# A recurrence in units of two head pairs by a quarter of the tokens, with r, k and v kept in DRAM

## The chip, the cores and the metric

The kernel runs on one core of a Trainium2 chip. The time is device microseconds for one execution; the smaller, the better. The profile follows one execution instruction by instruction on the engines PE (matrix multiply; PEld is its weight load), DVE (VectorE), ACT (ScalarE), POOL (GpSimd) and SP (SyncE, which here only issues DMAs). Every engine works through its own queue of instructions in order.

## The reference

One layer over 1024 tokens of width 1024: a normalised and modulated input `h`, one wide projection, two groups of heads side by side, a gate on each, and an output projection. The first group is a recurrence over the tokens with a 64 x 64 state for each of 8 heads; the second is causal attention with low-rank queries, keys and values.

```python
h = rms_norm(x, norm_g) * (1 + scale) + shift
proj = h @ w_in
# 8 heads of 64: r, k, v, decay w, kk (normalised k) and a from proj
def step(state, inp):
    sa = einsum('bhvk,bhk->bhv', state, kk_t)
    state = state * w_t - sa * (kk_t * a_t) + v_t * k_t
    y = einsum('bhvk,bhk->bhv', state, r_t)
# group norm of y per head, + (r k r_k) v; attention heads beside it
y = concat([y_rwkv * silu(gate_r), y_mla * silu(gate_m)])
out = rms_norm(x + gate * (y @ w_out), final_g)
```

## The kernel before

**Stages.** (1) Loads, normalisation and modulation; the modulated input is held transposed as a high and a low part (`hTh`, `hTl`), and three tiles of the projection (the low-rank columns, k and r of the first head pair) are formed as it arrives. (2) The other 24 tiles of the input projection, with the recurrence woven between them. (3) `values`: value, rotary query and first key and query tiles for the attention. (4) Attention over four head pairs. (5) Output projection, final norm, stores.

**A projection tile** (`proj`, `mm3`) is 128 columns by 1024 tokens, made in two halves of 512 tokens. A half is 8 contraction blocks of three matmuls of 512 columns (high x high, high x low, low x high; lines 159 to 161, tile `mm`), in one of two PSUM banks. Afterwards an evacuation empties the bank: for r, k and v that is `evac_shift` (ACT line 211, DVE lines 212 and 218), which mixes each token with the one before it. In the kernel before, it writes tiles of its own (`rkv_`, six buffers for r and k, four for v) that stay in SBUF until the recurrence reads them. Others go through `etile`, three shared buffers of 128 x 512, and from there by DMA to DRAM.

**The recurrence in chunks.** It is not run token by token. A unit is one head pair by 512 tokens, so there are 8 units (4 pairs, 2 halves), each of 8 chunks of 64 tokens. For a unit, `prep` builds decays and scaled keys, `products` multiplies them (tile `gps`, line 552), `invert` inverts the triangular part of each chunk on DVE with 62 short instructions (lines 600, 602) between two trips through DRAM, `tmat` completes the inverse (`y1ps`, `y2ps`), and `turn_kb` and `turn_v` turn the operands. Then `chain` steps through the 8 chunks, and `post` normalises and gates what it gave.

**A step of the chain** is serial. First leg: X from the state (line 668), copied by ACT (672). Second leg: the inverse times X (679), two negating copies on ACT (685, 686); the old state goes through an identity matmul into the new one's bank (682). Third leg: the keys' part is added (690), and two scaled copies on ACT (693, 694) put the next state into `ST`. The output `Y` gets its two parts from lines 676 and 696. "Two" stands for the two heads of the pair, which lie on partitions 0 to 63 and 64 to 127. A step handles one chunk of one pair, so 64 steps follow in all; the chains of the four pairs don't depend on each other, but run one after another.

**What sets the order.** The main loop has 11 rounds `n` of `STEPS[n]` places. Tables give the place at which each piece of work is emitted (`PREP`, `PROD`, `TURN`, `TMAT`, `POST`); one leg of the chain is emitted at each place; and `RATE[n]` pieces of projection (one contraction block, three matmuls) go into each place from the generator `filler`, which takes the tiles in the order of the list `tiles` and then `values`. Unit n is prepared in round n, turned in round n+1, stepped through in round n+2, and finished in round n+3. A scheduler then orders the instructions of each engine by this order of emission, raised for evacuations (`first`) and for the chain's ACT copies (`quick`).

Of the kernel before, what the change touches and what calls it, by code (L numbers as in the profile page):

```python
# [17 lines left out]
F32 = mybir.dt.float32  # L18
# [4 lines left out]
ALU = mybir.AluOpType  # L23
# [4 lines left out]
P = 128  # L28
# [19 lines left out]
BKR = 6  # L48
BV = 4
# [8 lines left out]
PREP = ((0, 0, 1, 2, 3, 5, 5, 7), (4, 4, 5, 6, 7, 9, 9, 11), (9, 9, 10, 11, 12, 14, 14, 16))  # L58
PROD = ((8, 13), (12, 15), (17, 21))
TURN = (2, 5, 6)  # L60
POST = (1, 1, 5, 5, 8)
TMAT = ((13, 15), (14, 15), (15, 17))
EVAC = 120
STEPS = (16, 16, 24, 24, 24, 24, 24, 24, 24, 24, 9)
RATE = (2.3, 2.3, 2, 2, 2.2, 2, 2, 2, 1.7, 0.4, 1)
# [17 lines left out]
def hymba_kernel(ctx: ExitStack, tc: tile.TileContext, x, pos, cols, cst, winit, w_ada, b_gate, w_in, w_lora, w0,  # L83
# [38 lines left out]
    d_bv = [dram.tile([P, S], F32, name=f"d_bv{p}") for p in range(NP)]  # L122
    d_y = [dram.tile([P, S], F32, name=f"d_y{p}") for p in range(NP)]
# [63 lines left out]
    rkv = {}  # L187
# [11 lines left out]
    def evac_shift(ti, dest):  # L199
# [4 lines left out]
        def f(h, ps):  # L204
            if dest is None:
                o = etile("pst")
            else:
                o = (vp if dest[1] == "v" else rkvp).tile([P, HALF], F32, tag="v" if dest[1] == "v" else "kr", name=f"rkv_{dest}_{h}",
                              bufs=BV if dest[1] == "v" else BKR)
                rkv[dest + (h,)] = o  # L210
# [8 lines left out]
            if dest is None:  # L219
                hs = slice(h * HALF, (h + 1) * HALF)  # L220
                A.activation(LW[0:64, hs], o[0:64], AF.Tanh)
                A.copy(LW[64:128, hs], o[64:128])
# [18 lines left out]
    GROUP = [(O_LORA, evac_shift(12, None)), (RW, evac_shift(4, (0, "k"))), (0, evac_shift(0, (0, "r")))]  # L241
# [103 lines left out]
    def shift_tile(p, nm):  # L345
        ti = {"r": 0, "k": 4, "v": 8}[nm] + p
        return proj(ti * P, P, evac_shift(ti, (p, nm)))
# [113 lines left out]

    def prep(un):

        p, h = un["p"], un["h"]
        hs = slice(h * HALF, (h + 1) * HALF)
        cp = slice(p * P, (p + 1) * P)
        r, k = (rkv.pop((p, n, h)) for n in "rk")
        wl = tm.tile([P, P], F32, tag="wl", name="wl", bufs=2)
        SY.dma_start(wl[:], w_lora[:, cp])
        w0b = tm.tile([P, P], F32, tag="w0b", name="w0b", bufs=2)  # L470
        SY.dma_start(w0b[:], w0[:, cp].to_broadcast([P, P]))
        sq = t2("sq", (P, HALF))
        A.activation(sq[:], k[:], AF.Square, scale=col("k_k", p))
# [3 lines left out]
        T.matmul(aps[:], lhsT=wl[64:128], rhs=LW[64:128, hs], start=True, stop=True)  # L477
        for i in range(4):
            T.matmul(ps[:, i, :], lhsT=LW[0:64, h * HALF + i * P:h * HALF + (i + 1) * P], rhs=wl[0:64],
                     start=True, stop=True)  # L480
        z = t2("z", (P, 4, P))
        V.tensor_tensor(z[:], ps[:], w0b[:, None, :].to_broadcast([P, 4, P]), ALU.add)
        ta = t2("ta")
        A.activation(flat(ta), aps[:], AF.Tanh, scale=0.5, bias=a0h[:, p:p + 1])
# [15 lines left out]
        V.tensor_scalar(kw[:], ta[:], kah[:, p:p + 1], kam[:, p:p + 1], ALU.mult, ALU.add)  # L500
# [12 lines left out]
        yield  # L513
        ps = psA.tile([P, HALF], F32, tag="rp", name="kps")
# [3 lines left out]
        V.scalar_tensor_tensor(flat(kn), k[:], col("k_k", p), ps[:], ALU.mult, ALU.mult)  # L518
# [8 lines left out]

        V.scalar_tensor_tensor(flat(kw), r[:], col("r_k", p), flat(kw), ALU.mult, ALU.mult)
# [4 lines left out]
        V.tensor_tensor(kb[64:128, :, 1, :], kn[64:128], Ei[64:128], ALU.mult)  # L533
        yield
        ps = psA.tile([P, HALF], F32, tag="rp", name="bps")
        T.matmul(ps[:], lhsT=cs("blk"), rhs=flat(kw), start=True, stop=True)
        v = rkv.pop((p, "v", h))
        bv = t2("bv0", (P, HALF))
        V.tensor_tensor(bv[:], ps[:], v[:], ALU.mult)
        SY.dma_start(d_bv[p][:, hs], bv[:])  # L540
        un.update(eL=eL, rq=rq, kb=kb, v=v, GA=[[None, None], [None, None]])
        yield

    def products(un, q):

        p, h, kb, rq = un["p"], un["h"], un["kb"], un["rq"]
# [7 lines left out]
        dn = d_n[2 * p + h][:].rearrange("(s q c b) i j -> s q b i c j", s=2, q=2, b=2)  # L554
# [33 lines left out]
    def invert(un):  # L588

        i = 2 * un["p"] + un["h"]  # L590
# [16 lines left out]
    def fetch(un):  # L607

        i = 2 * un["p"] + un["h"]
        TT = un["TT"] = TTs[un["h"]]  # L610
# [37 lines left out]
    @contextmanager  # L648
    def quick(un):
        with tc.high_priority(offset=QUICK[un["p"] == NP - 1]):  # L650
            yield

    def chain(un, nxt):

        p, h = un["p"], un["h"]
# [3 lines left out]
        if h == 0:  # L659
            G.memset(ST[0:64, 0, 0, :], 0.0)  # L660
            G.memset(ST[64:128, 0, 1, :], 0.0)
        rcs = psA.tile([P, 2, 3, C], F32, tag="rc", name="rc", bufs=1)
        Y = un["Y"] = psA.tile([P, 8, C], F32, tag="ry", name="Y", bufs=1)
        for c in range(8):
            ps = rcs[:, c % 2]
            last = c == 7 and nxt is None
            for s in range(2):
                T.matmul(ps[rows[s], 0, :], lhsT=GA[s][c // 4][:, c % 4, 0:C], rhs=ST[:, c, s, :],  # L668
                         start=True, stop=True)
            X = ch.tile([P, C], F32, tag="X", name="X", bufs=2)  # L670
            with quick(un):
                A.copy(X[:], ps[:, 0, :])
# [240 lines left out]
    def filler():  # L913
        ws = [tiles[0][0]()]
        gr, tb = gate_row(), tables()
        for i, (_, steps) in enumerate(tiles):
# [5 lines left out]
            if i == 11:  # L922
                yield from scale_ckv()
# [411 lines left out]
```

## Time and profile before

| | us |
|---|---|
| three runs, median | 945.38 (942.20 to 951.51) |
| the profiled execution's own time | 947.39 |
| its span, first to last instruction | 945.6 |
| PE busy in it | 850.4 (90%) |
| DVE busy | 576.5 (61%) |
| ACT busy | 476.7 (50%) |
| POOL busy | 294.1 (31%) |

A busy PE is one with a matmul in flight, not one at its peak. A row of the timeline gives the start in us from the span's start, the time from first to last moment of the instructions that it merges, the engine, the line, and what was written and read; an engine's idle time ahead of it stands in brackets with what released it. A matmul of f32 data counts as two instructions, so that `x4` is two matmuls. The spacing from one row's start to the next is what a matmul costs in a row of others, since they overlap.

### The profile page before, as it was taken

What the parts mean: (1) busy time and instruction counts of PE and PEld (TensorE: products, weight loads), DVE (VectorE), ACT (ScalarE), POOL (GpSimd) and SP (SyncE); (2) the same over time, 40 slices, a digit from 0 to 9 for tenths busy, and PEclk for the clock granted to TensorE, in tenths of its full rate; (3) what the DMA queues carried; (4) which work ended last, traced back from release to release, by engine and by line L of the source; (5) the groups of instructions that cost most, each with busy time, mean ns of one, the idle gap of its engine ahead of it and who ended that gap; (6) DMA issues with size and microseconds to landing.
All of it is one profiled execution on the core that took longest, in us unless ns stands there. A gap on an engine that the chain in (4) does not pass through costs nothing.

```text
span 945.6 us, 16387 instructions
## 1 busy us (share of the span) xinstructions
PE 850.4 (90%) x5828; PEld 638.6 (68%) x5828; DVE 576.5 (61%) x1438; ACT 476.7 (50%) x1132; POOL 294.1 (31%) x355
## 2 busy tenths in 40 slices
PE   1799998999889999999999899896899998989897
PEld 1587776776667567667776666663677777868685
DVE  5796484293863855936636736462678778764333
ACT  2656131535635535445435444564688788762311
POOL 2314131133222322412325130323346454464300
PEclk9999998799999999999999999797899999999899
DMA  8762313124413424232332543335202031026133
GB/s 270 228 183 73 84 29 87 57 68 107 143 37 98 138 68 124 72 81 86 90 85 63 140 123 87 113 103 150 54 26 71 26 101 57 1 89 223 56 115 130
DMA packets 116737, 93.01 MB, mean 98 GB/s; under 512 B 38952, under 2 KB 92464, under 8 KB 116656
## 3 DMA queue, kind: packets, MB, share of 16 engines
q1 hardware_dynamic: 115696, 88.82, 32.0%
q0 software_dynamic: 960, 3.15, 1.4%
q8 instruction: 46, 0.75, 0.3%
q14 instruction: 35, 0.29, 0.1%
HBM read 69.12 MB, written 22.81 MB: 97 GB/s over the span
## 4 chain that ended last, share of the span: by engine, by line
PE 54%; DVE 17%; ACT 9%; DMA 7%; issue 5%; POOL 5%; SPq 1%; POOLq 0%; DVEq 0%; ACTq 0%
PE mm L159 8%; PE mm L160 6%; PE mm L161 6%; DVE W L602 3%; DVE wtmp L600 3%; DMA wor<-in_w_out 2%; PE tp L1052 2%; ACT pr L1041 2%; PE gps L552 2%; PE po L1114 2%; PE po L1116 2%; PE po L1115 2%; PE Y L676 2%; ACT PTh L1061 1%; PE rc L668 1%
## 5 line engine op out<-in xcount | busy, mean ns | idle before, releaser
L159 PE MATMUL mm<-hTh,whi 128*128 128x512 f32 (+1 forms) x384 | 171.8, 447 | 1.9 <-DVE tg L230 1.9
L160 PE MATMUL mm<-hTl,whi 128*128 128x512 f32 (+1 forms) x384 | 154.2, 402 | 0.0
L161 PE MATMUL mm<-hTh,wlo 128*128 128x512 f32 (+1 forms) x384 | 154.2, 401 | 0.0
L152 POOL TENSOR_TENSOR wlo<-wraw,whi 128x512 fp32r<-128x512 f32 (+1 forms) x54 | 69.8, 1293 | 206.8 <-ACT whi L151 192.3
L159 PEld LDWEIGHTS mm<-hTh,whi 128*128 128x128 f32 (+1 forms) x384 | 72.3, 188 | 23.6 <-issue 2.3
L161 PEld LDWEIGHTS mm<-hTh,wlo 128*128 128x128 f32 (+1 forms) x384 | 72.3, 188 | 17.8
L160 PEld LDWEIGHTS mm<-hTl,whi 128*128 128x128 f32 (+1 forms) x384 | 72.8, 190 | 12.4 <-issue 1.4
L1045 POOL TENSOR_SCALAR pr<-pr,sm 128x512 f32<-128x512 f32 (+2 forms) x96 | 55.2, 584 | 77.4 <-DVE sm L1042 50.0
L602 DVE TENSOR_TENSOR W<-W,wtmp 128x60 f32<-128x60 f32 (+24 forms) x248 | 68.8, 277 | 6.0
L600 DVE TENSOR_TENSOR wtmp<-W,N 128x60 f32<-128x60 f32 (+24 forms) x248 | 66.1, 267 | 7.0 <-DMA N<-d_n 0.9
L1041 ACT ACTIVATE pr<-sp,mx,rss 128x128 f32<-128x128 f32 (+3 forms) x64 | 53.3, 833 | 15.4 <-DVE mx L1034 13.0
L1062 DVE TENSOR_TENSOR PTl<-tp,PTh 128x512 fp32r<-128x512 f32 (+2 forms) x96 | 52.4, 554 | 12.2 <-ACT PTh L1061 10.1
L151 ACT CAST whi<-wraw 128x512 fp32r<-128x512 f32 (+1 forms) x54 | 32.6, 605 | 51.6 <-PE mm L160 45.1
L1033 DVE TENSOR_REDUCE mx<-sp 128x1 f32<-128x128 f32 (+3 forms) x64 | 48.0, 750 | 13.4 <-PE sp L1027 13.3
L1114 PE MATMUL po<-wo,yh 128*128 128x512 f32 x128 | 51.7, 404 | 3.9 <-DVE xo L1247 3.1
L1061 ACT CAST PTh<-tp 128x512 fp32r<-128x512 f32 (+2 forms) x96 | 44.0, 477 | 14.4 <-PE tp L1052 10.6
L1115 PE MATMUL po<-wo,yh 128*128 128x512 f32 x128 | 51.2, 400 | 0.0
L1116 PE MATMUL po<-wo,yl 128*128 128x512 f32 x128 | 51.2, 400 | 0.0
L1052 PE MATMUL tp<-cstt,pr 128*128 128x128 f32 x288 | 44.9, 278 | 4.4 <-POOL pr L1045 2.1
L1073 PE MATMUL op<-PTh,Vt 128*128 128x256 f32 (+1 forms) x160 | 41.9, 292 | 5.1 <-ACT od L1088 5.1
L685 ACT ACTIVATE ST<-rc 64x64 f32<-64x64 f32 x64 | 13.8, 215 | 52.7 <-PE rc L682 44.7
L1023 PE MATMUL sp<-kt,qt 96*128 96x512 f32 (+2 forms) x96 | 36.4, 379 | 4.2 <-ACT pr L1041 4.2
(394 smaller groups left out, 1974.7 us busy)
## 6 DMA issues: line engine op xcount, KB each, us to landing
wraw<-in_w_in SPq DMA_DIRECT2D x52, 256.0 KB, 3.0
wa<-in_w_ada SPq DMA_DIRECT2D x64, 128.0 KB, 3.4
xt<-in_x SPq DMA_DIRECT2D x8, 512.0 KB, 5.8
wg<-in_w_ada SPq DMA_DIRECT2D x32, 128.0 KB, 2.2
N<-d_n SPq DMA_DIRECT2D x32, 128.0 KB, 2.8
wor<-in_w_out SPq DMA_DIRECT2D x16, 256.0 KB, 2.9
cr<-d_c SPq DMA_DIRECT2D x14, 256.0 KB, 2.8
d_c<-craw SPq DMA_DIRECT2D x10, 256.0 KB, 2.6
```

The lines of the kernel that those rows point to most:

```text
L152: G.tensor_tensor(lo[:, :, :m], raw[:, :, :m], hi[:, :, :m].bitcast(F32), ALU.subtract)
L159: T.matmul(ps[:m], lhsT=hi[:, k % 4, :m], rhs=a, start=first, stop=False)
L160: T.matmul(ps[:m], lhsT=hi[:, k % 4, :m], rhs=b, start=False, stop=False)
L161: T.matmul(ps[:m], lhsT=lo[:, k % 4, :m], rhs=a, start=False, stop=last)
L600: V.tensor_tensor(t, W[:, 0:n, u:u + 1].to_broadcast([P, n, m]), N[:, u:u + 1, u + 1:32].to_broadcast([P, n, m]), ALU.mult)
L602: V.tensor_tensor(W[:, 0:n, u + 1:32], W[:, 0:n, u + 1:32], t, ALU.subtract)
L1041: A.activation(pr[:, 0:n], sp[:, 0:n], AF.Exp, scale=rss[:, i:i + 1], bias=mx[:], accum_out=sm[:])
L1045: G.tensor_scalar(pr[:, a:e], pr[:, a:e], sm[:], 1.0, ALU.mult, ALU.mult)
L1052: T.transpose(tp[:, j, :], pr[:, (j0 + j) * P:(j0 + j + 1) * P], ident)
L1114: T.matmul(ps, lhsT=yh[k][:, ts_], rhs=hi, start=first, stop=False)
L1115: T.matmul(ps, lhsT=yh[k][:, ts_], rhs=lo, start=False, stop=False)
L1116: T.matmul(ps, lhsT=yl[k][:, ts_], rhs=hi, start=False, stop=last)
```

## The change

A unit becomes two head pairs (group `g`) by 256 tokens (quarter `t`). It still has 8 pieces of work of a pair and a chunk, but `chain` now takes four steps of two pairs each: every leg does both chunks that stand at the same place in the two pairs, four heads side by side. The state has a tile of its own, `S`, next to its copy in `ST`; identity matmul and first part of `Y` read it and moved into the third leg. A leg is emitted at every second place, and the first four units are pairs 0 and 1, the last four pairs 2 and 3.

A unit now needs only a quarter of r, k and v, but of two pairs at once. So `evac_shift` writes them through the shared `etile` buffers to DRAM (`d_rkv`), and `load_rkv` fetches the quarter of both pairs when `prep` (k, later r) and the new `bonus` (v) want it. The third tile formed with the arriving input is k of pair 1. The list `tiles` becomes r0, r1, v0, v1, two gates, k2, k3, r2, r3, v2, v3, two kv latents, the rotary key, two gates, three q latents, four gates. The tables of places are rewritten.

```diff
-BKR = 6
-BV = 4
+BKR = 4
+BV = 2
...
-STEPS = (16, 16, 24, 24, 24, 24, 24, 24, 24, 24, 9)
-RATE = (2.3, 2.3, 2, 2, 2.2, 2, 2, 2, 1.7, 0.4, 1)
+QT_ = 256
+STEPS = (20, 20, 24, 24, 24, 24, 24, 24, 24, 24, 14)
+RATE = (2.3, 2.2, 1.69, 1.69, 1.69, 1.69, 1.69, 1.69, 1.69, 1.69, 1)
...
         def f(h, ps):
-            if dest is None:
-                o = etile("pst")
-            else:
-XX[dest + (h,)] = o
+            o = etile("pst")
...
+            hs = slice(h * HALF, (h + 1) * HALF)
+            if dest is not None:
+                SY.dma_start(d_rkv[dest][:, hs], o[:])
+                stored.add(dest + (h,))
...
+    def load_rkv(un, nm):
+        t = (vp if nm == "v" else rkvp).tile([P, 2 * QT_], F32, tag="v" if nm == "v" else "kr", name=nm,
+                                             bufs=BV if nm == "v" else BKR)
+        for a, p, aq in pairs(un):
+            SY.dma_start(t[:, aq], d_rkv[nm, p][:, un["ts"]])
+        return t
...
+        for i in range(4):
+            last = i == 3 and nxt is None
+            cc = [a * 4 + i for a in range(2)]
+            for a in range(2):
+                for s in range(2):
+                    T.matmul(ps[rows[s], 0, a, :], lhsT=GA[s][a][:, i, 0:C], rhs=ST[:, cc[a], s, :], start=True, stop=True)
+            X = ch.tile([P, 2, C], F32, tag="X", name="X", bufs=2)
             with quick(un):
-                A.copy(X[:], ps[:, 0, :])
+                A.copy(X[:], ps[:, 0])
             yield
+            for a in range(2):
+                for s in range(2):
+                    T.matmul(ps[rows[s], 1, a, :], lhsT=TT[rows[s], cc[a], :], rhs=X[rows[s], a, :], start=True, stop=True)
+            with quick(un):
+                A.mul(ST[lo, i:8:4, 0, :], ps[lo, 1], -1.0)
+                A.mul(ST[hi, i:8:4, 1, :], ps[hi, 1], -1.0)
+            yield
+            for a in range(0 if last else 2):
+                for s in range(2 if Sv else 0):
+                    T.matmul(ps[rows[s], 2, a, :], lhsT=ident[rows[s], rows[s]], rhs=Sv[rows[s], a, :],
+                             start=True, stop=False)
+                for s in range(2):
+                    T.matmul(ps[rows[s], 2, a, :], lhsT=KB[:, s, cc[a], :], rhs=ST[:, cc[a], s, :],
+                             start=Sv is None, stop=True)
...
+                        for s in range(2):
+                            A.mul(dst[rows[s], a * 4 + n, s, :], ps[rows[s], 2, a, :], eL[rows[s], cc[a]:cc[a] + 1])
+                    for a in range(2):
+                        A.mul(Sn[:, a], ps[:, 2, a], eL[:, cc[a]:cc[a] + 1])
+            for a in range(2):
+                for s in range(2 if Sv else 0):
+                    T.matmul(Y[rows[s], cc[a], :], lhsT=rq[rows[s], cc[a], 1, :], rhs=Sv[rows[s], a, :],
+                             start=True, stop=False)
                 for s in range(2):
+                    T.matmul(Y[rows[s], cc[a], :], lhsT=GA[s][a][:, i, C:2 * C], rhs=ST[:, cc[a], s, :],
+                             start=Sv is None, stop=True)
...
-    tiles = [shift_tile(0, "v"), shift_tile(1, "k"), shift_tile(1, "r"), shift_tile(1, "v")]
-    tiles += latent(1, O_CKV, 2, 3) + [gate_r(0)] + [shift_tile(2, n) for n in "krv"]
-    tiles += [gate_r(1), krope(), gate_r(2)] + [shift_tile(3, n) for n in "krv"]
-    tiles += latent(0, O_CQ, 3, 0) + [gate_r(3)] + [gate_m(i) for i in range(4)]
+    tiles = [shift_tile(p, n) for n in "rv" for p in range(2)] + [gate_r(0), gate_r(1)]
+    tiles += [shift_tile(p, n) for n in "krv" for p in (2, 3)] + latent(1, O_CKV, 2, 3)
+    tiles += [krope(), gate_r(2), gate_r(3)] + latent(0, O_CQ, 3, 0) + [gate_m(i) for i in range(4)]
...
-            if rec is not None:
+            if rec is not None and j % 2 == 0:
                 next(rec, None)
```

What the change moves on PE, in the order of its queue. First a stretch of the chain in stage 2, before the change. Each row is a run of matmuls of one line; `x2` is the two heads of a pair.

```order
L668 MATMUL rc<-ST,GA 64x64 x2
L676 MATMUL Y<-ST,rq 64x64 x2
L159 MATMUL mm<-hTh_125,whi 128x512
L160 MATMUL mm<-hTl_133,whi 128x512
L161 MATMUL mm<-hTh_125,wlo 128x512
L159 MATMUL mm<-hTh_118,whi 128x512
L160 MATMUL mm<-hTl_126,whi 128x512
L161 MATMUL mm<-hTh_118,wlo 128x512
L679 MATMUL rc<-X,TT_815 64x64 x2
L682 MATMUL rc<-ST,cstt 64x64 x2
```

And a third leg of the changed kernel, between two projection matmuls:

```order
L166 MATMUL mm<-hTh_136,wlo 128x512
L709 MATMUL rc<-S,cstt 64x64 x2
L712 MATMUL rc<-ST,KB 64x64 x2
L709 MATMUL rc<-S,cstt 64x64 x2
L712 MATMUL rc<-ST,KB 64x64 x2
L725 MATMUL Y<-S,rq 64x64 x2
L728 MATMUL Y<-ST,GA 64x64 x2
L725 MATMUL Y<-S,rq 64x64 x2
L728 MATMUL Y<-ST,GA 64x64 x2
L164 MATMUL mm<-hTh_137,whi 128x512
```

First and second leg are now one run of four matmuls each (`rc<-ST,GA x4`, `rc<-X,TT x4`), and the third is a block of eight runs in which lines 709 and 725, which use half the array's rows, take turns with 712 and 728, which use all of them. Over stage 2 and 3, PE's queue goes from projection-like matmuls of 512 columns to small ones and back 200 times before and 161 times after; inside these blocks of small matmuls the kind changes 287 times before and 371 times after. The matmuls are 4576 before and 4568 after.

The second place is the end of stage 3. Before, the last unit's chain reaches nearly to the first scores of the attention (`sp`); its last rows are these, with the rows of its `post` (line 723) behind them.

```order
L786 MATMUL qkps<-ckvl_6001,wkh 128x512
L787 MATMUL qkps<-ckvh_5999,wkl 128x512
L679 MATMUL rc<-X,TT_816 64x64 x2
L785 MATMUL qkps<-ckvh_6000,wkh 128x512
L786 MATMUL qkps<-ckvl_6002,wkh 128x512
L696 MATMUL Y<-ST,GA 64x64 x2
L787 MATMUL qkps<-ckvh_6000,wkl 128x512
L723 MATMUL ytps<-cstt,ys 64x128 x8
L785 MATMUL qkps<-cqh_5411,wqh 128x512
```

In the changed kernel the last rows of the chain stand in the first third of that stage:

```order
L902 MATMUL vps<-wvl,ckvh_6008 128x512
L903 MATMUL vps<-wvh,ckvl_6010 128x512
L728 MATMUL Y<-ST,GA 64x64 x2
L725 MATMUL Y<-S,rq 64x64 x2
L728 MATMUL Y<-ST,GA 64x64 x2
L823 MATMUL qrps<-cqh_5718,wrh 128x512
L824 MATMUL qrps<-cql_5721,wrh 128x512
```

Behind the last projection matmul (`mm`) stood 11 of the 64 steps' first legs (line 668); now 2 of the 32 (line 694) stand there. Between the chain's last row and the rows of its `post` lie 1 matmul before and 63 after. The completion of the last unit's inverse (`y1ps`, `y2ps`) has moved ahead of the last projection matmul.

The third place is SP's queue. Here k of pair 2 goes out and comes back; the issue of the load (line 474) stands behind the store (line 221), and that behind its evacuation.

```order
L482 DMA wl<-in_w_lora 128x256
L221 DMA d_k_80<-pst 128x512
L484 DMA w0b<-in_w 128x256
L155 DMA wraw<-in_w_in 128x4x128 x2
L221 DMA d_k_80<-pst 128x512
L474 DMA k<-d_k_80 128x256
```

Before, these rows had no store and no load of k, r and v. SP's queue has 566 DMAs before and 670 after: 24 stores of 256 KB, 48 loads of 128 KB, and 32 more because the recurrence's bonus, gate and output move in quarters.

More of the change, by code (lines that the diff above doesn't have):

```diff
@@ L122, in hymba_kernel @@
     d_bv = [dram.tile([P, S], F32, name=f"d_bv{p}") for p in range(NP)]
+    d_rkv = {(n, p): dram.tile([P, S], F32, name=f"d_{n}{p}") for n in "rkv" for p in range(NP)}
     d_y = [dram.tile([P, S], F32, name=f"d_y{p}") for p in range(NP)]
@@ L186, in hymba_kernel @@
     vp = pool(top, "vp", side="right")
-    rkv = {}
+    stored = set()
     def etile(nm):
@@ L658, in chain @@
         rows = (lo, hi)
[L659 to L662, printed above, removed]
-        Y = un["Y"] = psA.tile([P, 8, C], F32, tag="ry", name="Y", bufs=1)
[L664 to L670, printed above, removed]
+        Sv = un.get("S")
@@ L684, in chain @@
-            with quick(un):
-                A.mul(ST[lo, c, 0, :], ps[lo, 1, :], -1.0)
-                A.mul(ST[hi, c, 1, :], ps[hi, 1, :], -1.0)
-            yield
-            if not last:
-                for s in range(2):
-                    T.matmul(ps[rows[s], 2, :], lhsT=KB[:, s, c, :], rhs=ST[:, c, s, :], start=False, stop=True)
-                dst, cn = (ST, c + 1) if c < 7 else (nxt["ST"], 0)
-                with quick(un):
-                    A.mul(dst[lo, cn, 0, :], ps[lo, 2, :], eL[lo, c:c + 1])
-                    A.mul(dst[hi, cn, 1, :], ps[hi, 2, :], eL[hi, c:c + 1])
@@ L695, in chain @@
-            for s in range(2):
-                T.matmul(Y[rows[s], c, :], lhsT=GA[s][c // 4][:, c % 4, C:2 * C], rhs=ST[:, c, s, :],
-                         start=False, stop=True)
+            for a in range(2):
[4 more added lines that the diff above has]
+                A.mul(ST[hi, i:8:4, 1, :], ps[hi, 1], -1.0)
@@ L719, in post @@
         for q in range(2):
-            last = p == NP - 1 and h == 1
+            last = un["n"] == 7
+            p = 2 * un["g"] + q
             ps = (psM if last else psA).tile([64, 4, P], F32, tag="mm" if last else "rt", name="ytps")
@@ L880, in hymba_kernel @@
     cpool, Vt, b1 = {}, None, None
-    units = [dict(p=i // 2, h=i % 2) for i in range(8)]
+    units = [dict(n=i, g=i // 4, t=i % 4, ts=slice(i % 4 * QT_, (i % 4 + 1) * QT_)) for i in range(8)]
     def gate_row():
@@ L931, in late @@
     def late(n):
-        return 2 if 2 <= n <= 6 else int(n == 1)
+        return min(n, 2) + (n == 7)
     def after(n):
```

145 lines of the change are left out of this document (82 added, 63 removed).

## The prediction

> **What bounds the kernel now.** I read first the clock and span, then the busy times cut at the borders of the stages, then PE's timeline inside them, then the waits.
>
> ```profile
> core 0: 945.6 us, clock 0.962
> ```
> ```profile
> core 0: us, PE busy (x) PEld busy (x) DVE busy (x) ACT busy (x) POOL busy (x), PEclk, DMA share, GB/s
> 62.00:166.00 104.00, 94.50 (x531) 74.53 (x528) 64.02 (x153) 38.75 (x66) 29.34 (x28) 0.97 0.27 69
> 166.00:591.00 425.00, 408.03 (x3248) 286.68 (x3247) 254.76 (x718) 202.65 (x522) 115.13 (x108) 0.97 0.33 92
> 591.00:665.00 74.00, 60.99 (x464) 42.02 (x463) 31.45 (x64) 39.80 (x110) 22.33 (x31) 0.84 0.40 118
> 665.00:946.00 281.00, 251.87 (x1432) 208.80 (x1431) 181.12 (x401) 167.14 (x390) 112.89 (x168) 0.97 0.25 80
> ```
>
> From 62 us (the end of the first three tiles) to 591 (the last projection matmul) PE is busy 502.5 of 529 us; DVE, ACT, POOL and the DMA engines are far from full (255, 203 and 115 of 425 us, share 0.33). This stage is PE's, and 26.5 us of it are idle. The 74 us from 591 to 665, the first scores, are different: PE is idle for 13 us and its granted clock is 0.84. The first 62 us and the 281 us from the scores on hold nothing that the change touches; I leave them as they are. So the change has a stage of 603 us to work on, and there it must either take work from PE, or waits, or clock.
>
> What the chain costs PE is seen in the timeline of one step:
>
> ```profile
> 576.93 0.40 PE L161 MATMUL mm<-hTh,wlo 128*128 128x512 f32 x1
> 577.26 0.33 PE L679 MATMUL rc<-X,TT 64*64 64x64 f32 x4
> 577.42 0.28 PE L682 MATMUL rc<-ST,cstt 64*64 64x64 f32 x4
> 577.63 0.50 PE L159 MATMUL mm<-hTh,whi 128*128 128x512 f32 x1
> 577.97 0.39 PE L160 MATMUL mm<-hTl,whi 128*128 128x512 f32 x1
> 578.20 0.40 PE L161 MATMUL mm<-hTh,wlo 128*128 128x512 f32 x1
> 578.53 0.34 PE L690 MATMUL rc<-ST,KB 128*64 128x64 f32 x4
> 578.69 0.29 PE L696 MATMUL Y<-ST,GA 128*64 128x64 f32 x4
> 578.91 0.50 PE L159 MATMUL mm<-hTh,whi 128*128 128x512 f32 x1
> ...
> 580.50 0.34 PE L668 MATMUL rc<-ST,GA 128*64 128x64 f32 x4
> 580.76 0.33 PE L676 MATMUL Y<-ST,rq 64*64 64x64 f32 x4
> 581.02 0.50 PE L159 MATMUL mm<-hTh,whi 128*128 128x512 f32 x1
> ```
>
> Two projection matmuls start 0.23 us apart (577.97, 578.20). Going over to small ones takes 0.33, so 0.10 more; the first projection matmul after them has 0.34 to the next, 0.11 more. A run of a pair takes 0.16 to the next run of the same kind (577.26 to 577.42, both 64*64; 578.53 to 578.69, both 128*64), 0.26 to one of the other kind (580.50 to 580.76), and 0.21 to 0.26 to a projection matmul. So a leg costs 0.10 + 0.16 + 0.21 + 0.11 = 0.58 us (line 679), 0.59 (690) and 0.73 (668), 1.90 a step, 122 us in all 64. PE waits little here: between the rows there is almost nothing left.
>
> **PE's work: term 0.** The matmuls stay (4576 and 4568). Twice as many in a leg would halve the entries, but the order of PE shows how far that goes: 200 blocks of small matmuls become 161, so 39 x (0.10 + 0.11) = 8 us less; inside them the kind changes 371 instead of 287 times, since the third leg takes turns between 64 and 128 rows, so 84 x 0.10 = 8 us more. The bounds: by legs alone, a third leg costs 0.10 + 7 x 0.26 + 0.22 + 0.11 = 2.25 and a double step 0.59 + 0.58 + 2.25 = 3.42, 32 of them 109, and 13 us are won; if the entries don't pay and the changes do, 8 are lost. I take 0, as the whole order is nearer to the truth than one leg.
>
> The Trainium skill's page "TensorEngine Tiling (Array Packing)", section "Key Properties", has a rule against this change: switching the tiling mode, not merely the tile, drains TensorE. The trace agrees, with 0.26 us against 0.16. Without that rule the seven changes in a third leg would cost 0.70 us less, and the sum would be 32 x 0.70 = 22 us lower; by it, the zero above holds.
>
> **Waits in the main part: -8.** The list of PE's waits from 62 to 592:
>
> ```profile
> PE rc L668 <- ACT ST L694: 4.9, 5, 2.1
> PE gps L552 <- DVE kb L532: 4.5, 2, 3.2
> PE rc L679 <- ACT X L672: 1.5, 1, 1.5
> PE rc L690 <- ACT ST L686: 1.0, 1, 1.0
> ```
>
> Columns are total, times, longest. The chain's own waits for ACT are 7.4 us; shorter ones within the modelled spans may double that. Half as many legs remain, each with twice the projection between it and the next: six matmuls, 1.4 us, become about ten, 2.3 us. The copies that the next leg waits for grow, from two of 0.31 to four, with two more for `S` behind them:
>
> ```profile
> L693 ACT ACTIVATE ST<-rc,eL 64x64 f32<-64x64 f32 x60 | 18.4, 307 | 37.7 <-PE rc L690 37.2
> ```
>
> That is 1.2 us instead of 0.6, still under 2.3, with the Y runs of about 1 us ahead of it too. I take 8 us off; the bounds are 0 (every wait returns) and -15. The waits for DVE (`gps`, 4.5 us for `kb` alone) stay, as products and inverse are the same.
>
> **r, k, v through DRAM: 0, up to +22.** Stores and loads are off PE's path while they are early enough.
>
> ```profile
> L211 ACT ACTIVATE rkv_(1, 'k')_0_1024<-mm,omu x1: 687/687/687, 105.3 to 105.3; 128x512 f32<-128x512 f32 x1
> L212 DVE SCALAR_TENSOR_TENSOR rkv_(1, 'k')_0_1024<-mm,colt,rkv_(1, 'k')_0_1024 x1: 749/749/749, 106.0 to 106.0; 128x511 f32<-128x511 f32 x1
> d_c<-craw SPq DMA_DIRECT2D x10, 256.0 KB, 2.6
> cr<-d_c SPq DMA_DIRECT2D x14, 256.0 KB, 2.8
> ```
>
> A shared buffer is held for 0.69 + 0.75 + 2.6 = 4.0 us, and a half tile takes PE at least 24 x 0.23 = 5.5 us: the second PSUM bank and three buffers cover it. Queued behind a store on SP are weight loads (`wraw`), asked for a whole tile, 2 x 5.5 = 11 us, ahead, and the trips of the inverse. If the cover goes, PE waits for a PSUM bank; rival C prices that. The new wait is ACT's: `prep` asks for k and squares it (`sq`) at the same place, 2.8 us apart, and behind `sq` on ACT stand the chain's copies. If ACT stood still for every load, that were 8 x 2.8 = 22 us; nothing if the scheduler, which knows of the load, keeps `sq` back. In PE's order the projection between two legs, 2.3 us, covers most of one such wait, so I take 0.
>
> **The end, 591 to 665: -31, of which 14 come back.** Now its rows:
>
> ```profile
> 590.70 0.39 PE L161 MATMUL mm<-hTh,wlo 128*128 128x512 f32 x1
> ...
> 648.35 0.50 PE L787 MATMUL qkps<-ckvh,wkl 128*128 128x512 f32 x1
> 657.09 1.92 PE L723 MATMUL ytps<-cstt,ys 128*64 128x128 f32 x8 [8.23 <-POOL ys L717]
> ```
> ```profile
> 659.96 0.63 PE L786 MATMUL qkps<-cql,wqh 128*128 128x512 f32 x1
> 660.39 0.63 PE L787 MATMUL qkps<-cqh,wql 128*128 128x512 f32 x1
> ...
> 664.66 0.22 PE L1023 MATMUL sp<-kt,qt 96*128 96x128 f32 x1
> ```
>
> The last unit's chain runs to 648; its norm then keeps PE's queue waiting 8.2 us, and afterwards matmuls start 0.43 us apart (659.96, 660.39) instead of 0.23. In the changed order 63 matmuls lie between the chain and that norm, 63 x 0.23 = 14 us, more than the 8.7 from 648.35 to 657.09; so this wait and the slow stretch after it go. Of the chain, 11 of 64 steps stood here, 11 x 1.90 = 21 us; now two third legs and their neighbours, 2 x 3.42 + 1 = 8. With the inverse's last part moved too, about 14 us of PE work pass from the end into the main part; they are not won.
>
> What is left in the end: first the value weights, which can only be fetched when the projection has freed their room.
>
> ```profile
> 594.44 0.92 SPq L774 DMA_DIRECT2D wvr<-in_w_v x2
> 597.59 1.43 POOL L777 TENSOR_SCALAR wvr<-wvr,colt 128x512 f32<-128x512 f32 x2 [1.08 <-DMA wvr<-in_w_v]
> 607.57 0.79 PE L863 MATMUL vps<-wvh,ckvh 128*128 128x512 f32 x1
> ```
>
> They are scaled at 599.0; with one more copy that is 9.5 us after 590.7 (it was 17 to the first `vps` at 607.57, ACT being held by the chain). Then 105 of the 114 wide matmuls, 24 us of PE, but DVE must split every result: it is busy 31.45 us in this window (row 591 to 665), nearly all of it such work, so I take 30 us. With the last evacuation and some half clock 3.5. Sum 9.5 + 30 + 3.5 = 43 us against 74. The bounds: 36, if PE sets the pace, and 52, if evacuations wait as now.
>
> **Sum.** Last projection matmul: 590.7 + 14 (moved in) - 8 (waits) + 0 = 597. First scores: 597 + 43 = 640 instead of 665, so 25 us less. The profiled execution's own time is 947.4 around a span of 945.6, 0.2% above the median 945.4; I set the gain against the median: 920 us. A measurement of this kernel tells about 1%, 9.5 us, from no change.
>
> **Rivals.**
> (A) More is won: every chain wait goes (-15), the end is paced by PE (36), and with few idle stretches the low clock goes too. 590.7 + 14 - 15 - 10 + 36 = 616, 49 less: 896. For it: PEclk 0.84 in the end and 0.97 before, the latter worth 3% of 529, 16 us, at most. Against: the waits for DVE, which start the main part's longest idle stretches, stay. The Trainium skill, "TensorE: Matmul & The Clock Gate", section "What's actually happening", states two clocks, full and half, the half one after an idle window of about 3.4 us; the spacing of 0.43 us after the 8.23 us idle agrees. By it the end's shorter idle brings 3 or 4 us, which the 43 already hold.
> (B) The end shrinks but the main part takes it: 14 us come in, the chain's waits return in longer blocks with six ACT copies in a third leg, and DVE's waits grow. 590.7 + 14 + 8 + 47 = 660: 5 less, 940. For it: PE is 95% busy, and its work doesn't fall.
> (C) Slower: stores through three buffers. While the rotary tables are made, two of the three `etile` buffers are held, and just then k2 to v3, twelve halves, are evacuated through one. That decides once a buffer is held longer than a half's share of the main part (529 us over the 48 halves of 24 tiles, 11 us). SP's queue can do it:
>
> ```profile
> SPq L605 <- DVE W L602: 20.4, 5, 11.0
> ```
>
> One store queued behind a wait of up to 11.0 us holds its buffer for 15 us, 4 too long; twelve such halves are 48 us: 920 + 48 = 968. Against: only five such waits are listed.
> (D) The change doesn't do what it says: PE's order shows the legs doubled, but 161 blocks where 192 legs became 96. This is in the zero above and gives no time of its own.
>
> **Numbers.** Forecast 0.64 (about 906 to 934), A 0.12, B 0.14, C 0.10. Faster by over 1% is forecast and A, 0.76; within 1% is B, 0.14; slower is C, 0.10. The range reaches from a little above A to past B, 902 to 943.
>
> **What would show it.** Right: the last projection matmul near 597, first scores near 640; no wait of PE for the norm's `ys` before `ytps`; third legs of about 2.2 us; chain waits for ACT below 5 us. Wrong: the projection ending past 605 (B); PE waiting for an evacuation with `pst`, or SP's stores far behind DVE (C); scores more than 50 us after the last projection (evacuations still pace the end).

## The result and the profile after

The changed kernel takes 939.6 us (median of 19 runs, 929.8 to 947.6) where the kernel before takes 948.6 in the runs beside it: ratio 0.9903, with an interval of 0.9878 to 0.9929. A second series gave 0.9948 (0.9909 to 0.9987). So the change wins 5 to 9 us where 25 were forecast; 939.6 lies inside the range of 902 to 943, but the gain is a fifth to a third of the forecast, and the time is that of rival B.

The stages of the changed kernel, cut at the same events (the end of the first three tiles, the last projection matmul, the first scores):

```profile
core 0: us, PE busy (x) PEld busy (x) DVE busy (x) ACT busy (x) POOL busy (x), PEclk, DMA share, GB/s
62.00:166.00 104.00, 93.50 (x469) 75.68 (x468) 61.90 (x152) 37.38 (x65) 29.52 (x28) 0.93 0.41 120
166.00:608.00 442.00, 429.10 (x3521) 311.51 (x3519) 259.48 (x749) 218.97 (x552) 122.33 (x107) 0.95 0.39 109
608.00:657.00 49.00, 41.22 (x238) 30.43 (x236) 29.59 (x58) 25.62 (x61) 17.87 (x26) 0.90 0.61 173
657.00:939.00 282.00, 251.60 (x1431) 208.10 (x1429) 181.26 (x399) 166.90 (x389) 114.04 (x169) 0.96 0.25 79
```

The last stage is what it was (282 us, 281 before). The end shrank from 74 to 49 us and its clock rose from 0.84 to 0.90. But the main part grew from 529 to 545 us, and there the clock fell, from 0.97 and 0.97 to 0.93 and 0.95. The two borders, in PE's timeline:

```profile
607.38 0.39 PE L166 MATMUL mm<-hTh,wlo 128*128 128x512 f32 x1
...
647.91 0.77 PE L823 MATMUL qkps<-cqh,wqh 128*128 128x512 f32 x1 [2.98 <-DVE kt L843]
...
656.59 0.22 PE L1064 MATMUL sp<-kt,qt 96*128 96x128 f32 x1
```

607.4 was forecast as 597, and 656.6 as 640. PE's waits from 62 us to the last projection matmul (total, times, longest):

```profile
PE gps L577 <- DVE W L627: 5.6, 1, 5.6
PE gps L577 <- DVE kb L554: 2.7, 2, 1.5
PE mm L164 <- DVE wtmp L625: 2.3, 1, 2.3
PE nps L509 <- ACT sq L487: 2.1, 1, 2.1
...
PE Y L725 <- ACT S L722: 1.3, 1, 1.3
PE Y L728 <- ACT ST L703: 1.1, 3, 0.4
...
PE rc L694 <- ACT S L722: 0.9, 1, 0.9
...
PE rc L709 <- ACT ST L704: 0.2, 1, 0.2
```

The chain's waits for ACT are 1.3 + 1.1 + 0.9 + 0.2 = 3.5 us, 7.4 before. The long ones are those of `gps` for DVE: 5.6 + 2.7 and two shorter groups, 1.8 and 1.6, 11.7 us in all, where the kernel before has 12.2 (its list has 4.5, 3.8, 2.0 and 1.9).

**Where the clock fell.** A third leg in the timeline, and what follows it:

```profile
251.41 0.40 PE L166 MATMUL mm<-hTh,wlo 128*128 128x512 f32 x1
251.74 0.33 PE L709 MATMUL rc<-S,cstt 64*64 64x64 f32 x4
252.00 0.34 PE L712 MATMUL rc<-ST,KB 128*64 128x64 f32 x4
...
253.58 0.34 PE L728 MATMUL Y<-ST,GA 128*64 128x64 f32 x4
253.84 1.05 PE L509 MATMUL nps<-cstt,sq 128*128 128x2 f32 x8
254.76 0.58 PE L164 MATMUL mm<-hTh,whi 128*128 128x512 f32 x1
255.13 0.63 PE L165 MATMUL mm<-hTl,whi 128*128 128x512 f32 x1
255.56 0.63 PE L166 MATMUL mm<-hTh,wlo 128*128 128x512 f32 x1
```

The leg takes 2.10 us (251.74 to 253.84), as forecast, and the eight `nps` matmuls of two columns 0.92. Nothing waits. Yet from 255 us projection matmuls start 0.43 us apart (255.13, 255.56) instead of 0.23. The same stretch, and one like it, cut into windows of 3.4 us:

```profile
251.60:255.00 3.40, 3.40 (x42) 2.73 (x42) 3.40 (x13) 2.39 (x7) 0.00 (x0) 1.00 0.85 239
255.00:258.40 3.40, 3.40 (x9) 2.34 (x8) 3.40 (x14) 0.00 (x0) 1.65 (x1) 0.50 0.63 178
309.60:313.00 3.40, 3.40 (x43) 2.59 (x42) 3.36 (x12) 2.80 (x8) 1.79 (x1) 1.00 0.52 168
313.00:316.40 3.40, 3.40 (x10) 2.60 (x9) 3.16 (x11) 0.62 (x1) 2.69 (x2) 0.50 0.30 78
```

PE is busy for all of the first window (3.40 of 3.40), with 42 matmuls that are nearly all small; in the window after it the clock is 0.50. So half clock came without any idle time in the profile's spans (whose ends are modelled). Between 62 us and the last projection matmul the granted clock is half for 58 us of the changed kernel, 31 of the one before (55 and 34 in a second profile of each).

**PE's time, split.** For each step from one matmul's start to the next I took the usual step of that pair of kinds at full clock (the fifth part of all such steps is shorter); an excess under 0.12 us counts as work too, what half clock adds up to as much again as half clock, and the rest as waits. Two profiles of each kernel, in us:

| from 62 us | PE's time | work | half clock | waits |
|---|---|---|---|---|
| to the last projection: before | 528.7, 529.3 | 475.6, 474.2 | 10.2, 12.1 | 42.9, 43.3 |
| to the last projection: changed | 545.4, 545.1 | 485.4, 485.1 | 21.8, 20.2 | 38.3, 39.9 |
| to the first scores: before | 602.7, 600.7 | 527.4, 525.9 | 16.4, 16.8 | 58.7, 58.0 |
| to the first scores: changed | 594.6, 595.8 | 520.7, 520.4 | 26.3, 25.9 | 47.5, 49.5 |

By this the change took 6 us of work and 10 of waits, and half clock took back 9 of the 16. Differences of a few us in one part are not certain: waits under 0.12 us stand in "work". With a shortened inverse on DVE (below) the same matmuls of the changed kernel show 11 us less work.

### The profile page after: what moved, and what is told of

The parts are those of the page before. It is cut to its first block, busy times and chain, and to the rows that moved or that the text cites. A ratio compares the mean times of both kernels' runs of the same rounds, so it can differ in the third digit from the quotient of the medians.

```text
span 939.0 us, 16568 instructions
## 1 busy us (share of the span) xinstructions
PE 852.4 (91%) x5812; PEld 654.2 (70%) x5812; DVE 576.8 (61%) x1462; ACT 477.4 (51%) x1112; POOL 298.7 (32%) x351
## 4 chain that ended last, share of the span: by engine, by line
PE 62%; DVE 14%; ACT 11%; DMA 5%; issue 4%; POOL 2%; SPq 1%; DVEq 0%; POOLq 0%; ACTq 0%
PE mm L164 10%; PE mm L165 8%; PE mm L166 8%; ACT pr L1082 3%; PE gps L577 2%; DMA wor<-in_w_out 2%; DVE wtmp L625 2%; ACT PTh L1102 2%; PE tp L1093 2%; DVE W L627 2%; PE po L1155 2%; PE po L1157 2%; PE po L1156 2%; PE rc L694 1%; PE Y L728 1%
## 5 line engine op out<-in xcount | busy, mean ns | idle before, releaser
L164 PE MATMUL mm<-hTh,whi 128*128 128x512 f32 (+1 forms) x384 | 169.5, 441 | 3.2 <-DVE wtmp L625 2.3
L166 PE MATMUL mm<-hTh,wlo 128*128 128x512 f32 (+1 forms) x384 | 158.7, 413 | 0.0
L165 PE MATMUL mm<-hTl,whi 128*128 128x512 f32 (+1 forms) x384 | 158.6, 413 | 0.0
L164 PEld LDWEIGHTS mm<-hTh,whi 128*128 128x128 f32 (+1 forms) x384 | 74.2, 193 | 24.4 <-issue 3.2
L166 PEld LDWEIGHTS mm<-hTh,wlo 128*128 128x128 f32 (+1 forms) x384 | 74.6, 194 | 18.3
L625 DVE TENSOR_TENSOR wtmp<-W,N 128x60 f32<-128x60 f32 (+24 forms) x248 | 69.4, 280 | 5.5
L720 ACT ACTIVATE ST<-rc,eL 64x64 f32<-64x64 f32 x120 | 37.1, 309 | 46.7 <-PE rc L712 45.1
L1103 DVE TENSOR_TENSOR PTl<-tp,PTh 128x512 fp32r<-128x512 f32 (+2 forms) x96 | 52.4, 553 | 12.1 <-ACT PTh L1102 9.8
```

The lines of the kernel that those rows point to most:

```text
L164: T.matmul(ps[:m], lhsT=hi[:, k % 4, :m], rhs=a, start=first, stop=False)
L165: T.matmul(ps[:m], lhsT=hi[:, k % 4, :m], rhs=b, start=False, stop=False)
L166: T.matmul(ps[:m], lhsT=lo[:, k % 4, :m], rhs=a, start=False, stop=last)
L625: V.tensor_tensor(t, W[:, 0:n, u:u + 1].to_broadcast([P, n, m]), N[:, u:u + 1, u + 1:32].to_broadcast([P, n, m]), ALU.mult)
```

## The experiments

Theory 1: the clock holds the gain back, since longer runs of small matmuls make PE stream too little, that is, take in too few columns. Theory 2: PE is not what bounds the main part; its work, when it goes, comes back as waits for DVE (and as clock, as an effect). Theory 3: only the changes of kind in the third leg cost. Times are medians; the kernel before took 945 to 947 us in the runs beside each, by which the changed kernel stands at 937 to 941.

**The third leg by kinds.** The edit, in the third leg:

```
-            for a in range(0 if last else 2):
-                for s in range(2 if Sv else 0):
-                    T.matmul(ps[rows[s], 2, a, :], lhsT=ident[rows[s], rows[s]], rhs=Sv[rows[s], a, :],
+            if Sv and not last:
+                for s in range(2):
+                    T.matmul(ps[rows[s], 2, :, :], lhsT=ident[rows[s], rows[s]], rhs=Sv[rows[s], :, :],
                              start=True, stop=False)
+            for s in range(2 if Sv else 0):
+                T.matmul(Y[rows[s], cc[0], :], lhsT=rq[rows[s], cc[0], 1, :], rhs=Sv[rows[s], 0, :],
+                         start=True, stop=False)
...
+            for s in range(2 if Sv else 0):
+                T.matmul(Y[rows[s], cc[1], :], lhsT=rq[rows[s], cc[1], 1, :], rhs=Sv[rows[s], 1, :],
+                         start=False, stop=True)
```

> The changed kernel with the third leg in another order: one matmul of 128 columns for the identity times S of both pairs, then Y of pair 0 with S, the four with KB, the four Y with GA, and last Y of pair 1 with S: two changes of kind in a leg instead of seven, 14 matmuls instead of 16. Theory 1 (the granted clock: stretches of 3.4 us in which PE streams for less than about a third, which the 2.2 us blocks of small matmuls cause, are followed by half clock, and that ate some 10 us of the forecast): the leg falls to about 1.6 us, 32 x 0.6 = 19 us less work, and half-clock windows between 62 us and the last projection matmul fall from 17 to about 10, 5 us more: about 917 us. Theory 2 (the time went to the chain's waits for ACT's copies and for DVE, PE is not what bounds): what PE saves comes back as waits, at most 5 us less, about 935. Theory 3 (only the changes of kind): 19 us less at an unchanged number of half-clock windows, about 921.

Measured: 932.6 us, ratio 0.9862 (0.9818 to 0.9905), some 4 us under the changed kernel, with intervals that overlap. The leg fell from 2.10 to 1.35 us:

```profile
319.04 0.43 PE L709 MATMUL rc<-S,cstt 64*64 64x128 f32 x4
...
320.39 0.50 PE L164 MATMUL mm<-hTh,whi 128*128 128x512 f32 x1
```

PE's work to the first scores fell by 22 us (520.7 to 498.5), so changes of kind do cost what their rows say; but waits rose by 18 (47.5 to 65.8), and half clock to the last projection matmul, which Theory 1 expected to fall, did not (65 us, 58 in the changed kernel). Theory 2 had 935. PE's list of waits in this kernel, and one of the waits on PE and on DVE:

```profile
PE gps L577 <- DVE W L627: 15.0, 4, 5.6
```
```profile
387.64 0.39 PE L166 MATMUL mm<-hTh,wlo 128*32 128x512 f32 x1
392.78 1.60 PE L577 MATMUL gps<-rq,kb 64*128 64x128 f32 x7 [4.74 <-DVE W L627]
```
```profile
390.18 0.68 DVE L553 SCALAR_TENSOR_TENSOR kn<-ta,kn 128x512 f32<-128x512 f32 x1
390.78 1.25 DVE L625 TENSOR_TENSOR wtmp<-W,N 128x42 f32<-128x42 f32 x1
391.96 0.68 DVE L554 TENSOR_TENSOR kb<-kn,Ei 64x512 f32<-64x512 f32 x1
392.56 0.19 DVE L627 TENSOR_TENSOR W<-W,wtmp 128x42 f32<-128x42 f32 x1
392.78 0.69 DVE L555 TENSOR_TENSOR kb<-kn,Ei 64x512 f32<-64x512 f32 x1
```

`gps` needs `kb`, and `kb` is made on DVE between the steps of the inverse (`W`, `wtmp`, lines 625 and 627): PE is done with what stands ahead of `gps` at 388 and DVE delivers at 392.8. A shorter leg only brings PE there sooner.

**Legs of one pair.** Each leg of the chain again for one pair of heads, six legs in a token step (`for a in range(2)` around the three legs, a `yield` behind each, one leg at every step of the recording).

> The changed kernel with the legs undone: each leg of one pair again (six legs a token step instead of three, one at every step of the recording), all else as changed (units of a quarter, r, k, v through DRAM, projection order). Theory 1 (clock): 96 more entries at 0.21 us, 20 us more work; the blocks are half as long, so half-clock windows in the main part fall from 17 to about 9 as before the change, 8 to 10 us less: about 950 us. Theory 2 (waits for ACT): the work rises by the same 20 us and the chain's waits with it, to 963 or more. If the doubling itself was worth nothing: 940.

Measured: 978.6, ratio 1.0325 (1.0285 to 1.0365). Work rose by 22 us (to 542.9), as expected, but half clock by 11 (to 37.2) and waits by 9 (to 56.2). Shorter blocks did not bring the clock back, which speaks against Theory 1 as I had put it; Theory 2 had 963 or more. Four heads side by side are worth some 40 us in this order of the work. Since before and after lie 5 to 9 apart, the rest of the change (the order, the separate `S` with its changes of kind, r, k and v through DRAM) costs most of that again; no run takes these apart.

**Y as a leg of its own.**

```
+            yield
             for a in range(2):
                 for s in range(2 if Sv else 0):
...
-            if rec is not None and j % 2 == 0:
+            if rec is not None and j % 3 < 2:
```

> The changed kernel with the Y matmuls as a leg of their own, so that projection matmuls come between the rc and the Y halves of the third leg (blocks of 1.1 us instead of 2.2). Theory 1 (clock): 32 more entries at 0.21 us are 7 us more work, half-clock windows fall from 17 to about 11, 6 us less: 936 to 942, clock above that of the changed kernel. Theory 2 (waits): the copies get no more cover than before, 7 us more: about 947, clock unchanged.

Measured: 949.6, ratio 1.0042 (1.0015 to 1.0068). Work rose by 4 us (to 524.7), half clock fell by 2 (to 24.3) and waits rose by 10 (to 57.6). Half of the block's length left the clock where it was: Theory 2's 947 is nearer.

**The clock by itself.** A kernel that leaves out the whole computation and only keeps PE at work, run once.

> Nothing of the reference is computed: only PE at work without a break, in sections of some 24 us with 14 us of wide matmuls between: three wide matmuls and then k narrow ones of two columns, k = 6, 8, 9, 10, 11, 13, 18; then runs of 64x64 quarters, of 128x64 halves, both in turn, and both in turn with one wide in nine. Theory 1: although PE never waits, the granted clock falls to half in the sections whose streaming share is under about a third of the time (k = 10 and above by 0.213 us streamed of 0.228 a wide one and 0.115 a narrow one), and stays full in those above. Theory 2: the clock falls only where PE waits for 3.4 us, so it stays full throughout.

Measured, in the sections with six narrow ones (which show as 12, each in two passes, so that wide ones have 0.68 of 2.03 us), and in the runs of quarters and of both kinds in turn:

```profile
32.00:75.00 43.00, 43.00 (x171) 39.81 (x169) 0.00 (x0) 0.00 (x0) 0.00 (x0) 0.50 0.00 1
...
585.00:612.00 27.00, 27.00 (x923) 26.98 (x922) 0.00 (x0) 0.00 (x0) 0.00 (x0) 1.00 0.02 4
...
667.60:698.00 30.40, 30.40 (x638) 24.83 (x638) 0.00 (x0) 0.00 (x0) 0.00 (x0) 1.00 0.01 3
```
```profile
28.67 0.94 PE L125 MATMUL pw<-xh 128*128 128x512 f32 x3
...
34.37 1.63 PE L125 MATMUL pw<-xh 128*128 128x512 f32 x3
```

PE is busy 43.0 of 43.0 us and its clock is 0.50 (the three wide ones at 34.4 us take 1.63 instead of 0.94); all seven sections with narrow matmuls behave so, those with small quarters and halves do not. So much of Theory 1 is shown: low density alone halves the clock. Its limit of a third is not tested by this run: the sections with six, eight and nine narrow ones were expected at full clock, but with two passes each all seven stream about a third of the time or less. Nor does the run show what a third leg does alone: 638 matmuls of 64 columns in 30.4 us are 1,340 columns a us, a third leg has 2,048 in 2.10 us, 975 a us. In twelve profiles of this case, between 62 and 600 us, windows of 3.41 us at full clock with under 2,640 columns (34% of the 7,680 that fifteen wide matmuls would stream) were followed by half clock in about three quarters of 96 cases, those with over 3,840 in one of some 1,400.

The Trainium skill, "TensorE: Matmul & The Clock Gate", section "What's actually happening", puts half clock behind an idle window of about 3.4 us. The stretches here are 3.4 us and its multiples, which agrees; but these windows are busy from end to end, so the measurement decides: a window in which PE never waits is also followed by half clock when too little streams in it.

**Later products.** Two tables of the step numbers:

```
-PREP = ((0, 0, 1, 2, 3, 15, 15), (4, 4, 5, 6, 7, 13, 13), (9, 9, 10, 11, 12, 14, 14), (0, 0, 1, 2, 3, 5, 5))
-PROD = ((17, 19), (15, 18), (17, 21), (9, 13))
+PREP = ((0, 0, 1, 2, 3, 15, 15), (4, 4, 5, 6, 7, 11, 11), (9, 9, 10, 11, 12, 13, 13), (0, 0, 1, 2, 3, 5, 5))
+PROD = ((17, 19), (16, 18), (18, 21), (9, 13))
```

> The changed kernel with two numbers of its step tables moved: the transposes kps of units 1 to 6 one or two steps earlier, the products gps of units 1 to 6 one step later where the table allows, so that 21 to 34 projection matmuls stand on PE between the two instead of 13 to 17 (DVE and POOL make kb out of kps in some 5 us meanwhile). Theory 2 as it stands after the run with the grouped leg (PE's time in the main part is set by the waits of gps for DVE's kb, 13 to 21 us, each with a half-clock stretch behind it, and work taken from PE comes back there): the waits of gps fall below 8 us, half clock by some 10 us, so about 925 where the changed kernel has 937. Theory 1 (small matmuls' density sets the clock, waits are an effect): the waits go but the clock and the time move by less than 4 us: 933 or more.

Measured: 925.5, ratio 0.9778 (0.9736 to 0.982), clock 0.963 to 0.973. Theory 2's number. The changed kernel and this one, cut at their first scores:

```profile
62.00:656.60 594.60, 563.42 (x4218) 417.22 (x4217) 350.56 (x958) 281.98 (x677) 169.35 (x160) 0.94 0.41 116
```
```profile
62.00:640.30 578.30, 549.41 (x4222) 404.90 (x4221) 350.37 (x959) 282.59 (x677) 166.56 (x160) 0.98 0.43 119
```

The same work (523.9) now takes 578.3 us to the first scores, 16 less: waits fell by 5 (to 42.4) and half clock by 14 (to 12.0). The clock that came back is worth more than the waits that went. The kernel before, whose `gps` waits are as long, was not run with such tables, so this doesn't show that the change alone pays these waits.

**Both.** The grouped leg with these tables, and with the tables moved further (`kps` another step earlier, `TMAT` two steps later):

> The grouped third leg and the moved kps and gps together. Theory 2 (PE's saved work was lost to the waits of gps): now the 22 us less work of the grouped leg show in full: some 18 us less than with the tables moved alone, about 908. If another wait (the chain's for ACT, the inverse) takes their place: within 6 us of the tables moved alone, about 920.

> The grouped third leg with the tables moved further: kps of units 2 to 6 two steps earlier than in the changed kernel, gps one step later, and the two parts of tmat (which waited for DVE's T) two steps later. If the 20 us that grouping saves on PE were lost to waits at single places of the order (gps, y1ps): about 912, 13 us under the tables alone (925). If the saving always comes back, since DVE's inverse and PE's order run in a loop: 922 or more.

Measured: 928.4 (0.9751 to 0.9842 of before) and 926.1 (0.9743 to 0.982). Grouping adds nothing to the tables: in the second, work is 25 us less than with the tables alone (499.2), waits 17 more (59.3) and half clock 7 more (18.9). My 908 and 912 were wrong; the saving comes back, not at one place but at many.

**k first.** The first group in the order k, k, low rank, with the tables and a later `TMAT`:

> The moved tables of the run at 925 us (third leg as in the changed kernel), with k's two tiles ahead of the low-rank tile in the first group, so that k is back from DRAM before nps needs it, and tmat one or two steps later. The wait of nps for sq (2.1 us at 87.7 us, a half-clock stretch of 6.8 us behind it) and the waits of y1ps for DVE (3.2 us) should go: 4 to 8 us less, about 919. If the early wait is hidden anyway (PE then waits for another operand at the same place): 925.

Measured: 929.2 (0.9783 to 0.9858 of before), no gain on 925.5. The early wait for k's way through DRAM did go (`nps` has a single wait there, 0.9 us for `ta`, and none for `sq`), but the time did not follow.

**A short inverse.** `for u in range(24, 31)` instead of `range(31)`, which leaves out 24 of the 31 steps, in the changed kernel, with the grouped leg, and in the kernel before:

> The changed kernel with 24 of the 31 steps of the inverse on DVE left out (about 8 x 13 us of DVE's work; the inverse is then not computed). If DVE's queue is what PE waits for at gps (kb stands between steps of the inverse): the waits for DVE fall from 13 to about 4 us, 10 to 15 us less: about 925. If the waits come from the place of gps after kps and not from the inverse: kb is made about 1 us earlier only, 3 to 5 us less: 933.

> The grouped third leg and the shortened inverse (24 of 31 steps left out, so the inverse is not computed). If DVE's queue took what the grouped leg saved on PE: about 908, 18 us under the shortened inverse alone. If not: within 6 us of it.

> The kernel before with 24 of the 31 steps of the inverse left out (the inverse is not computed), as in the changed kernel's run at 907 us. If the change's gain was held back by DVE's inverse, the old order, whose PE work between 62 us and the first scores is 6 us longer and whose end is longer, gains less from the short inverse: to about 930, so that the change is worth some 23 us where the inverse is short, as forecast, against 9 where it is whole. If the inverse costs both the same 30 us: about 916.

Measured: 907.1 (ratio 0.9564, 0.9505 to 0.9623), 890.0 (0.9408, 0.9359 to 0.9457) and 923.0 (0.9738, 0.9672 to 0.9805). The changed kernel, that with the grouped leg and the kernel before, cut at their first scores:

```profile
62.00:623.40 561.40, 535.27 (x4216) 399.87 (x4215) 267.70 (x575) 284.47 (x682) 171.87 (x162) 0.97 0.44 123
```
```profile
62.00:609.30 547.30, 518.17 (x4106) 389.57 (x4105) 260.78 (x576) 284.08 (x682) 170.83 (x162) 0.97 0.45 127
```
```profile
62.00:642.80 580.80, 552.75 (x4238) 395.91 (x4236) 258.24 (x549) 280.32 (x696) 169.10 (x166) 0.96 0.35 95
```

With 83 us less on DVE (350.56 in the changed kernel over the same stretch, 267.70 here) the changed kernel gains 30 us, where 10 to 15 and 3 to 5 were expected, though DVE is busy for only 59% of that stretch. The waits of `gps` for DVE fell as expected, from 11.7 us to 3.6; by the split, waits in all are 9 us less, half clock 13 and work 11. The grouped leg now counts: 17 us, the gain that Theory 2 expected (18), where it was worth some 4 and nothing before. And the change itself: by the ratios, 0.9564 over 0.9738 is 0.982, so it is worth 17 us where the inverse is short, against 5 to 9 where it is whole. That is neither of the two numbers expected (23 and 9), and with four runs of each it is uncertain by some 9 us, which takes in both: that the change gains more with a short inverse is likely, not shown. In the split: work 13.6 us less than before's (523.5 to 509.9), waits 5.6 less, half clock the same (13.5, 13.2): in these two profiles nothing comes back.

**Filler behind the third legs.**

```
+            for _ in range(4):
+                T.matmul(ps[:, 3].rearrange("p a c -> p (a c)"), lhsT=ident, rhs=cs("blk"), start=True, stop=True)
             Sv = Sn
```

> The changed kernel with four more matmuls on PE behind each third leg (128x128 constants into an unused corner of the chain's bank; they only keep PE streaming): 32 x 4 x 0.112 = 14 us more work. Theory 1 (a window of 3.4 us in which PE streams under a third of the time is followed by half clock, whatever caused it): half clock between 62 us and the last projection falls from 55 to 58 us to about 30, clock to 0.965 or more, 8 to 11 us back: 943 to 947. Theory 2 (only long waits lower the clock): clock unchanged near 0.955, 14 us more: about 953.

Measured: 976.6, ratio 1.0311 (1.0251 to 1.0371), clock 0.947 to 0.957. My price was wrong: each of the 128 goes through PE twice, 256 records 0.11 us apart, so 31 us more work (to 552.1); and the fillers ended up a few matmuls behind the legs. Half clock rose to 30.7. It does not tell whether density or waits make the changed kernel's stretches; it shows only that 31 us more work cost 35 to 39.

**The same kernels again.**

> The kernel before once more, unchanged, for a second profile. Between its first profile and that of the changed kernel the half-clock time differs by 22 us, over many runs the mean clocks differ by 0.002 only, some 3 us. If the first profile of before was one with little half clock: about 78 us of half clock over the span here (clock 0.958) against 72, time near 946. If the profile was typical: 72 us.

> The changed kernel once more, unchanged, for a second profile and as a control beside the two below. If the half clock of its first profile (clock 0.950) was more than its usual: clock near 0.957, half clock between 62 us and the last projection matmul near 45 us instead of 58, time about 938. The same stretches should stand behind the same places (third legs with nps, the wait of gps at 158 us) if they belong to the order of PE, and other ones if they are chance.

Measured: 945.1 with clock 0.962, and 943.3 (ratio 0.9948) with 0.953 in the profiled execution. Both second profiles are near the first ones: 55 us of half clock in the changed kernel's main part, where 45 would have made the first one's 58 an exception. Six of the changed kernel's nine stretches of half clock in the main part stand at the same places again, one of them here:

```profile
312.60:316.00 3.40, 3.40 (x42) 2.70 (x42) 3.28 (x13) 2.81 (x8) 1.91 (x1) 1.00 0.57 161
316.00:319.40 3.40, 3.40 (x9) 2.36 (x8) 3.23 (x11) 0.62 (x1) 2.58 (x2) 0.50 0.32 87
```

These six belong to the order of the work; the other three did not come again, and two new ones did.

## Why the prediction was wrong

The direction was right and the gain was too large by a factor of three to five. Point by point:

- **"This stage is PE's".** This step failed. 502 busy microseconds of 529 were read as a bound, so work and waits were summed with a fixed clock. The runs show a loop instead: PE feeds DVE (`kps` to `kn`, `kb`), DVE feeds PE (`gps`, the inverse, `T`), and where PE comes too soon it waits, often with a stretch at half clock behind, during which it is busy. Busy time hid both. 22 us less work on PE were worth some 4, 83 us less on DVE 30. The loop was there before the change too (`gps` waits 12.2 us before, 11.7 after), so it tells why PE's work is no measure of the time, and only in part why this change gained so little.
- **Half clock in the main part: not in the sum, measured +8 to +12 us in the profiles** (10.2 and 12.1 to 21.8 and 20.2; over all runs less, see below). Rival A knew the clock only as a gain. The sum looked for PE's low clock in the end only, and there it did cost less (6.2 to 4.5).
- **PE's work, term 0: right as far as the split can tell.** To the first scores it fell by 6 us, within -13 and +8. The grouped leg shows that the changes of kind, which were set against the fewer entries, do cost: 22 us for five of them and two matmuls a leg.
- **Waits, -8: mechanism right, size short.** The chain's waits for ACT went from 7.4 to 3.5 us; all waits to the last projection fell by 3 to 5.
- **r, k, v through DRAM: 0, right as far as PE's waits show.** `sq` behind k's load held PE 2.1 us once, and having k earlier won nothing. PE waited for an evacuation by line 212 for 0.3 us only; rival C did not happen.
- **Last projection 597, measured 607.4.** Of the 10.7 us late (596.7 by the sum), half clock is 11.6 and waits 3.4 (4.6 less instead of 8); work grew by 9.8 (475.6 to 485.4), 4 under the 14 moved in.
- **End 43, measured 49.2: mis-sized.** The first `vps` stood 10.7 us after the last projection (9.5 forecast). The rest is 38.5 us instead of 33.5, and the 30 us of DVE in it were the wrong pace: DVE is busy 26.0 of the 38.5. Two chain steps with waits for `S` (1.08 us) and `ST` (0.43) stand just ahead of it, with half clock from 616.8 us on for 6.8; later come a wait of 2.98 us for the split of `kt`, ending at 647.9, with half clock from 647.5 on for 3.4, and shorter ones for `y`, `Vt` and `qt`. The norm's wait of 8.2 us for `ys` is gone, as forecast.
- **Rival B** had the time (940) and its sign (the projection ending past 605 us), and not the reason: chain waits did not return in longer blocks and waits of `gps` for DVE did not grow.

What stays open: over 52 runs of before and 27 of the changed kernel the mean granted clocks are 0.958 and 0.956, so half clock differs by some 3.5 us there (79 to 83), which would cost about 2 us, against 15 to 21 in the profiled executions. The split of the profiles explains their own 5 to 8 us; over the many runs less of the missing gain is the clock's, and the cause of the rest is open. Nor is it shown apart whether the long third legs or the waits near them cause the changed kernel's stretches: the run made for that did not tell. And no run kept r, k, v on the chip in the new order, so that part alone was not tried.

## What to carry to other kernels

An engine that is 95% busy need not be the bound: shorten its work in one experiment and see whether the time follows before a sum is built on it. On TensorE look at what streams, not at what is busy, and cut the profile into windows of 3.4 us: runs of small or narrow matmuls and waits near each other can halve the clock for the next window or two, so a wait costs more than its length (the 2.1 us of `nps` had 6.8 us at half clock behind them). Where two engines feed each other, try moving the consumer's place in the order (here two small tables, 925.5 us, the fastest kernel here that computes the whole layer) before making either faster.

## What the runs showed of the hardware

- TensorE without a wait ran at half clock for 43 us on end when 0.68 of each 2.03 us were wide matmuls; runs of 64x64 matmuls, which use a quarter of the array, kept the full clock (27.0 us at 1.00).
- Changes of kind between small matmuls are dear: five of them and two matmuls less took a third leg from 2.10 to 1.35 us, and 22 us off PE's work in all.
- f32 matmuls of 128x128 and of two columns show as two records each, 0.11 us apart, so a filler cost twice its estimate.
